# Four modulation halves moved behind layer 0's last expert, five gate tiles moved from RWKV to S5

## The chip, the cores and the metric

The kernel runs on one core of a Trainium2 chip. The metric is the device time of one execution in microseconds, as the median of several runs. The engines are TensorE (PE, with its weight loads PEld), VectorE (DVE), ScalarE (ACT), GpSimd (POOL) and SyncE (SP), which issues nearly all the transfers.

## What is computed

Two layers of a network over 256 latent tokens and 256 context tokens of width 1024, then a norm. Cut to what matters here:

```python
def hybrid_layer(x, cx, c, c_ctx, mod_w, mod_b, ...):
    mod_x = jax.nn.silu(c) @ mod_w + mod_b          # 6 chunks of 1024
    mod_c = jax.nn.silu(c_ctx) @ mod_w + mod_b
    sh1, sc1, g1, sh2, sc2, g2 = jnp.split(mod_x[:, None, :], N_MOD, axis=-1)
    px = modulate(x, norm_mix, sh1, sc1) @ w_in     # four mixers and their gates
    ...
    ys_x = [hyena_mixer(...), s5_mixer(...), rwkv_mixer(...), mamba_mixer(...)]
    x = x + g1 * merge(ys_x, gate_x, w_branch, w_out)
    x = x + g2 * moe_ffn(modulate(x, norm_ffn, sh2, sc2), *moe)
    ...                                             # the same for the context, but in the last layer

def merge(ys, gate_cols, w_branch, w_out):
    gates = jax.nn.sigmoid(gate_cols)
    out = sum(gates[..., i * D_MODEL:(i + 1) * D_MODEL] * (ys[i] @ w_branch[i]) for i in range(N_BRANCH))
    return out @ w_out
```

The modulation of a layer depends on c and c_ctx alone, so it can be computed at any time before its use. The experts (moe_ffn) are 16, of which each token uses two.

## The kernel before

Weights come as tiles of 128 x 1024 float32 (512 KB), each by one transfer of SP (`raw`, L302 to L310), and most are split into two parts for the products: ScalarE casts the high part (`wh`, L299), VectorE subtracts it for the low part (`wl`, L300), and TensorE multiplies three times (L337).

A layer runs in stages. First RWKV: its solve (`DD`, `TB`, `AB`, L499 to L530) goes level by level, with products on TensorE and masks, sums and transposes on VectorE. Then a stretch with S5, Hyena and Mamba side by side (`XX,F` are products of S5). Then the merge, the output projection, and the 16 experts, each with eight loads for `mg` and `mup` and four for `mdn`; an expert's output `yo` goes to memory (Y2) by an indirect store of GpSimd (L1419), token by token. Lists that are too long would be finished in a loop (`For_i`, L1650) whose number of turns is read at L1649; here it has none, but all engines cross it together, and SP waits for every transfer to have landed. Behind it the combine reads Y2 back and adds it to x (L1919 to L1941).

Two kinds of work are spread as fillers over the mixers. Gate tiles ("g", L1298, 32 for a layer): a tile of `w_in`, 24 products of 128x256 in layer 1, a tanh, a store. Halves of the modulation ("m", L1243 to L1273): four loads of `modw`, 16 pairs of products `raw,c`, a copy to `m` (L1251), a load of one row of `modb` into `m`, two instructions `m,rows`, an output `mo` (L1273 or L1271), a store to MR. `m` and `mo` share a tag with k.nt = 2 buffers. The order of the fillers is written out by hand:

```python
NH, NM3 = (12, 8), (0, 0)
F1 = ('g'*25+'mmm','g'*23,)
F2 = ('gm'*12,'mmmg'*4,)
```

F1 is the order beside RWKV, F2 the one beside S5, Hyena and Mamba, one entry for each layer; what is left of the 32 gates follows at the end. NH bounds the halves of a layer: 12 in layer 0 (the eight that are left of its own, and four of layer 1), 8 in layer 1. Within the windows that these strings open, the order on each engine is set by a scheduler that simulates the engines, so that a filler's products stand between those of the mixers. The experts' loads take buffers in a pattern of 19 (MST), so that a load waits for the use of the one 19 before it.

Of the kernel before, what the change touches and what calls it, by code (L numbers as in the profile page):

```python
# [8 lines left out]
F32 = mybir.dt.float32  # L9
# [9 lines left out]
D = 1024  # L19
# [5 lines left out]
# tiles of 128 columns of w_in: Hyena, S5, RWKV (r, k, v, wd | ad), Mamba (z, x, B, C), gates, then gd | dt  # L25
# [48 lines left out]
NH, NM3 = (12, 8), (0, 0)  # L74
F1 = ('g'*25+'mmm','g'*23,)
F2 = ('gm'*12,'mmmg'*4,)
NQS = (2, 4)  # pairs of groups in a part of S5
# [3 lines left out]
# ---------------------------------------------------------------- constants of the shapes  # L81


def _cst():
# [16 lines left out]
    # N^T of two-token blocks, rows s, columns t; backward scans in partitions 0..63  # L101
# [15 lines left out]
    # places less 1024  # L117
# [3 lines left out]
    # a token's row in U, and in Y2 for its first and second expert; Y2's less that of the rows without a token  # L121
    c["tok"] = np.stack([tok + 1.0, tok, tok + 512.0, tok - 1024.0], 2).reshape(128, 16)
    # resets of the running sums at the ends of 64-token chunks
# [7 lines left out]
def _rows():  # L131
    """rows of the modulation in groups of 32 (context, latent; the bias in the first's third): to each token's stream, to latent"""
    half = np.r_[np.ones(64), np.zeros(64)]
    m = np.zeros((128, 2, 128))
    for p in range(0, 128, 32):
        m[p:p + 2, 0] = half, 1 - half
        m[p + 1, 1] = 1
    m[2] = 1
    return m.reshape(128, 256)
# [39 lines left out]
def pack(inp):  # L179
    """Lays the inputs out for the loads; no arithmetic on them."""  # L180
# [32 lines left out]
    # S5: rows (second index of a pair of groups, state), columns (part, direction, pair)  # L213
# [44 lines left out]
class K:  # L258
# [13 lines left out]
    def pool(self, es, name, bufs=1):  # L272
        """a pool on the side of the parts of a layer"""
        return es.enter_context(self.tc.tile_pool(name=name, bufs=bufs, side="right", reuse_waits="tile"))
# [4 lines left out]
    def stream(self, banks="abgabgab", weights="mggg", parts="mg"):  # L279
        """banks of PSUM and buffers of weights (as loaded, and in parts) that the following program takes in turn:  # L280
        parts of a layer that run beside each other have their own"""
        self.tags, self.wtags, self.ptags = banks, weights, parts or weights
        if RESET:
            self.turn = self.wturn = 0

    def banks(self, **n):
        """the banks of PSUM by tag"""
# [9 lines left out]
    # ---- float32 operands of the large products in two parts of 12 bits: a b = ah bh + al bh + ah bl  # L297
# [4 lines left out]
    def raw(self, ap):  # L302
        """1024 columns of weights"""
# [7 lines left out]
    def wsplit(self, ap, k):  # L311
        """the parts of 1024 columns of weights (k by 1024 / k)"""
# [18 lines left out]
    def tr(self, out, in_, base=0):  # L331
        """out = in_^T on the tensor engine"""
# [6 lines left out]
    def rsqrt(self, pool, out, x, tag):  # L339
        """out = x ** -0.5 by Newton's iteration from the exponent's half; x > 0, small tiles"""  # L340
# [11 lines left out]
    def proj(self, l, t, xm, c0, c1, n=128):  # L352
        """p^T of w_in's tile t: n columns in partitions, tokens c0..c1"""
# [6 lines left out]
    # ------------------------------------------------------------------ RWKV-7  # L360
    def rwkv(self, l, xm, pc, dtT, yT, ctx_out, beside):
        """yT[:, hp, :]: the mixer's output, channels in partitions; columns 0..255 context, 256.. latent.
        dtT: Mamba's dt, from the tile that has both's columns, with tokens in partitions"""
        v, s, g, c = self.v, self.s, self.g, self.c
        with ExitStack() as es:
# [23 lines left out]
            def shifted(ps, n, j, out):  # L389
                """p + (mean of its neighbours - p) mu"""  # L390
# [20 lines left out]
            lo = {0: 64, 1: 0}  # partitions of the solves  # L411
# [4 lines left out]
            own = {d: slice(lo[d], lo[d] + 64) for d in range(2)}  # columns of a direction in the pairs' matrices  # L416
# [8 lines left out]
            for hp in range(2):  # L425
# [3 lines left out]
                # kappa: k k_k over its norm in the head  # L429
# [7 lines left out]
                # block diagonal pairs, of directions or heads: -b~ and k~ against kappa~, and the solves' (later M)  # L437
# [5 lines left out]
                for st in range(2):  # L443
# [6 lines left out]
                    for d in range(2):  # L450
                        dh = 2 * d + hp
                        # decay in log, its running sum in each chunk, and W = exp of that
# [21 lines left out]
                        s.activation(cum, cum, AF.Exp, scale=-1.0)  # 1 / W  # L474
# [16 lines left out]
                        # products of a chunk's tokens, masked: rows k~ and b~ (b~ and k~ backward)  # L491
# [11 lines left out]
                    # (I - N)^-1 of every chunk, N = -tril(kappa~ beta~^T): pairs of blocks, doubling  # L503
# [8 lines left out]
                    def each(a, b, us=range(8)):  # L512
                        """a^T b of the pairs"""
# [18 lines left out]
                    # tokens in partitions: v above (below) the solves, kappa~, and [k~; -b~]  # L532
# [33 lines left out]
                    # per chunk: H' = W_T (M H + k~^T v - b~^T u0), and y's reading of H  # L566
# [15 lines left out]
                    # the states that chunks enter (block diagonal), the last one that of the next stream's first chunk  # L582
# [23 lines left out]
                    # y^T  # L606
# [10 lines left out]
                    # group norm over a head, bonus, gate  # L617
# [24 lines left out]
    def headscale(self, pool, sq, f, eps, is_max, ni):  # L642
        """(f * sum over a head of sq, with eps added or as its least) ** -0.5, over the head's partitions"""
# [18 lines left out]
    # ------------------------------------------------------------------ conv of three taps, channels in partitions  # L662
    def conv3(self, ps, out, w3, b, c0, c1):
        """ps holds columns c0..c1 (of one or both streams)"""
# [8 lines left out]
    def silu(self, x, t):  # L673
        """x = silu(x), with a scratch like it"""
# [4 lines left out]
    # ------------------------------------------------------------------ Mamba-2  # L679
    def mamba(self, es, l, xm, pc, yT, ctx_out, dtT):  # L680
# [4 lines left out]
        if True:  # L685
# [10 lines left out]
            # softplus = max(x, 0) + log1p(exp(-|x|)); log1p(e) = 2 atanh(e / (2 + e))  # L696
# [17 lines left out]
            # running sums within a stream: forward heads 0..3, backward 4..7  # L714
# [16 lines left out]
            # weights of the context's tokens in its last state  # L731
# [6 lines left out]
            for gr in range(2):  # L738
# [8 lines left out]
                # tokens in partitions  # L747
# [10 lines left out]
                # the context's last states, [n, (direction, head, p)]  # L758
# [11 lines left out]
                for st in range(0 if ctx_out else 1, 2):  # L770
                    # C B^T by pairs of tiles, rows j, columns i; masked for each direction
# [33 lines left out]
                # + d x  # L805
                v.scalar_tensor_tensor(yT[:, gr, y0:], X[:, y0:], col("md", gr), py[:, y0:], OP.mult, OP.add)
            # times silu(z), norm over the channels
# [28 lines left out]
    def sin_of(self, pool, out, x, tag, cos=None):  # L836
        """out = sin(x), cos = cos(x): x less its whole turns, taken off in three parts"""
# [20 lines left out]
    def exp_of(self, pool, out, x, tag):  # L858
        """out = exp(x) for small tiles: 2^k times a polynomial of the rest"""
# [13 lines left out]
        # 2^k in two factors  # L873
# [8 lines left out]
    # ------------------------------------------------------------------ Hyena  # L882
    def hyena_filter(self, l, pc, pool, H):
        """H: [frequency, tile, (cos, sin), channel] of the two-sided filters"""
# [87 lines left out]
    # ------------------------------------------------------------------ S5  # L972
    def s5_params(self, l, pool):
        """[state, (part, direction, pair)]: lambda_bar, (lambda_bar - 1) / lambda, the decay over a chunk of
        4 tokens, cos and sin of the angles of a token, and of 1, 2, .. 64 chunks"""
# [44 lines left out]
    def s5_setup(self, l, a, P, tmp, TM, F, TT, ct, R):  # L1020
        """Matrices of 4-token chunks of the pairs of part a: E tokens -> state at the chunk's end, F state that
        enters -> tokens, TT within the chunk; ct: turns of the state by chunk (cos, sin), R: its decay over a chunk."""
# [940 lines left out]
```

## Time and profile before

| | before |
|---|---|
| time, median of three runs | 2172.78 us (2167.97 to 2173.02) |
| span of the profiled execution | 2165.3 us (its own time isn't listed apart) |
| TensorE busy | 1970.2 us, 11290 instructions |
| VectorE busy | 1651.0 us, 3451 instructions |
| ScalarE busy | 985.5 us, 1571 instructions |
| GpSimd busy | 399.0 us, 502 instructions |
| transfers | 406.28 MB, 188 GB/s on the mean |

Times inside the trace count from the start of the span. Layer 0's experts end near 1160, layer 1's RWKV runs from about 1210 to 1490, its S5 stretch from 1490 to 1740. "PEclk" is the share of the full TensorE clock that was granted, 1.00 for 2.4 GHz and 0.50 for 1.2. Buffers' numbers are left out in the rows, so that several tiles have one name.

### The profile page before, as it was taken

Reading aid. Unit: us, or ns where it says so; the run is one execution under the profiler, and the core shown is the slowest. Engines: PE = TensorE matmul, PEld = TensorE weight load, DVE = VectorE, ACT = ScalarE, POOL = GpSimd, SP = SyncE. Lnnn points to the kernel's source line nnn. Section 1 sums busy time; section 2 is a strip of 40 time slices with the busy share of each in tenths; the row PEclk is TensorE's granted clock in tenths of the full one; section 3 lists DMA queues with packets and bytes.
Section 4 is the critical chain, followed back from the end, with each engine's and each line's share of the span. In section 5 each row is a group of like instructions: output and inputs, shape, how many; then the busy total and the mean of one; then the engine's idle time right before and its main releaser. Section 6 shows DMA issues by size and latency. Waiting matters only on the chain. (4 is left out here: it accounts for less than half of the span.)

```text
span 2165.3 us, 31795 instructions
## 1 busy us (share of the span) xinstructions
PE 1970.2 (91%) x11290; PEld 1504.7 (69%) x11290; DVE 1651.0 (76%) x3451; ACT 985.5 (46%) x1571; POOL 399.0 (18%) x502
## 2 busy tenths in 40 slices
PE   6999999889999899999995899899798878999994
PEld 2779889567666678777774689897575767555652
DVE  5575675478888777999996686776879776888895
ACT  3321322244344234777773332323434335777783
POOL 1000100033532322102213010100524221010100
PEclk9999999889999898999998899999898988999997
DMA  7221221533444845999993221312434394899981
GB/s 299 78 74 59 74 67 52 197 123 113 156 146 154 313 172 186 362 368 372 372 341 138 84 90 63 98 52 76 160 134 161 129 350 174 304 329 366 330 325 64
DMA packets 131915, 406.28 MB, mean 188 GB/s; under 512 B 18139, under 2 KB 30205, under 8 KB 131361
## 3 DMA queue, kind: packets, MB, share of 16 engines
q1 hardware_dynamic: 125778, 388.34, 50.6%
q0 software_dynamic: 5968, 15.80, 2.3%
q8 instruction: 92, 1.51, 0.3%
q14 instruction: 77, 0.63, 0.1%
HBM read 374.72 MB, written 34.61 MB: 189 GB/s over the span
## 5 line engine op out<-in xcount | busy, mean ns | idle before, releaser
L299 ACT CAST wh<-raw 128x1024 fp32r<-128x1024 f32 x528 | 553.0, 1048 | 537.9 <-PE bank L337 482.9
L300 DVE TENSOR_TENSOR wl<-raw,wh 128x1024 fp32r<-128x1024 f32 x528 | 642.6, 1231 | 146.4 <-ACT wh L299 143.1
L337 PE MATMUL bank<-xmh,wh 128*128 128x512 f32 (+2 forms) x896 | 338.3, 378 | 15.8 <-ACT wh L299 14.7
L337 PE MATMUL bank<-xmh,wl 128*128 128x512 f32 (+2 forms) x896 | 331.0, 370 | 15.4 <-DVE wl L300 15.4
L337 PE MATMUL bank<-xml,wh 128*128 128x512 f32 (+2 forms) x896 | 326.4, 365 | 0.0
L337 PEld LDWEIGHTS bank<-xmh,wh 128*128 128x128 f32 (+1 forms) x896 | 176.7, 197 | 54.2 <-ACT wh L299 19.2
L337 PEld LDWEIGHTS bank<-xmh,wl 128*128 128x128 f32 (+1 forms) x896 | 175.9, 196 | 51.6 <-DVE wl L300 22.2
L337 PEld LDWEIGHTS bank<-xml,wh 128*128 128x128 f32 (+1 forms) x896 | 176.5, 197 | 29.2 <-issue 6.2
L337 PE MATMUL bank<-wh,xx 128*64 128x512 f32 x512 | 168.1, 397 | 0.2 <-ACT wh L299 0.2
L1419 POOL DMA_INDIRECT Y<-yo,ri x32 | 43.4, 1357 | 420.4 <-DVE yo L1418 304.8
L337 PE MATMUL bank<-DD,TB 128*128 128x64 f32 (+1 forms) x848 | 111.5, 273 | 1.3 <-DVE TB L523 0.9
L337 PEld LDWEIGHTS bank<-DD,TB 128*128 128x128 f32 x848 | 106.3, 192 | 6.0 <-DVE DD L598 0.9
L337 PE MATMUL bank<-wl,xx 128*64 128x512 f32 x256 | 102.8, 402 | 1.3 <-DVE wl L300 1.1
L337 PE MATMUL bank<-wl,hh 128*112 128x512 f32 (+1 forms) x256 | 99.9, 396 | 0.0
L337 PEld LDWEIGHTS bank<-wh,xx 128*64 128x64 f32 x512 | 69.6, 136 | 43.1 <-issue 1.4
L337 PE MATMUL bank<-wl,xh 128*112 128x512 f32 x240 | 97.9, 408 | 0.2
L337 PE MATMUL bank<-wh,hl 128*112 128x512 f32 (+1 forms) x256 | 97.4, 400 | 0.5 <-DVE hl L300 0.2
L337 PE MATMUL bank<-wh,xl 128*112 128x512 f32 x240 | 94.8, 395 | 0.9 <-DVE xl L300 0.9
L337 PE MATMUL bank<-wh,xh 128*112 128x512 f32 x240 | 92.8, 395 | 0.8 <-ACT xh L299 0.8
L337 PE MATMUL bank<-wh,hh 128*112 128x512 f32 (+1 forms) x256 | 89.8, 397 | 1.1 <-ACT hh L299 1.1
L337 PE MATMUL bank<-raw,c 128*32 128x256 f32 x768 | 71.3, 423 | 18.6 <-DMA raw<-in_modw_dram 18.6
L337 PE MATMUL bank<-DD,AB 128*128 128x64 f32 x640 | 84.5, 275 | 0.7 <-DVE DD L510 0.7
(547 smaller groups left out, 3799.5 us busy)
## 6 DMA issues: line engine op xcount, KB each, us to landing
raw<-in_mg_dram SPq DMA_DIRECT2D x128, 512.0 KB
raw<-in_mup_dram SPq DMA_DIRECT2D x128, 512.0 KB
raw<-in_mdn_dram SPq DMA_DIRECT2D x128, 512.0 KB
raw<-in_win_dram SPq DMA_DIRECT2D x112, 512.0 KB
raw<-in_modw_dram SPq DMA_DIRECT2D x96, 512.0 KB
GT<-t SPq DMA_DIRECT2D x32, 256.0 KB
raw<-in_wbr_dram SPq DMA_DIRECT2D x16, 512.0 KB
G<-GT SPq DMA_DIRECT2D x8, 1024.0 KB
```

The source lines that it names most:

```text
L299: self.s.copy(hi, src)
L300: (eng or self.v).tensor_tensor(lo, src, hi, OP.subtract)
L337: self.t.matmul(out, lhsT=lhsT, rhs=rhs, start=start, stop=stop)
L1419: g.indirect_dma_start(out=Y2, out_offset=bass.IndirectOffsetOnAxis(ap=to, axis=0), in_=yo, in_offset=None, bounds_check=1023, oob_is_err= ...
```

## The change

NM3 is now the number of halves that are computed behind the last expert of layer 0, in front of the loop; with four there, four instead of eight are left for layer 1's fillers. These are both halves of chunks 2 and 3 of layer 1's modulation. Their loads take the places of the pattern behind the experts' loads, their `m` and `mo` the two buffers of a tag in the experts' pool. Of layer 1's gate tiles 18 instead of 23 stand beside RWKV, and ten instead of four in the written order beside S5. The four reads of Y2 stand in a loop of their own ahead of the combine, and a block for NM4 halves (none) moves.

```diff
-NH, NM3 = (12, 8), (0, 0)
-F1 = ('g'*25+'mmm','g'*23,)
-F2 = ('gm'*12,'mmmg'*4,)
+NH, NM3 = (12, 8), (4, 0)
+F1 = ('g'*25+'mmm','g'*18,)
+F2 = ('gm'*12,'ggm'*4+'gg',)
...
-    def moe(self, l, m, x, pool, nt, rows, tabl, U, Y2, e_f, fp, tmp, ready, after):
+    def moe(self, l, m, x, pool, nt, rows, tabl, U, Y2, e_f, fp, tmp, ready, after, last):
...
                 for _ in prev:
                     pass
+                self.ft = tmp
+                last()
...
             nov = self.nc.values_load(cnti[0:1, 0:1], min_val=0, max_val=16)
             with self.tc.For_i(0, nov, 1) as e:
...
-                left = dict(g=32, m=NH[l] - (NM4 if last else 0))
+                left = dict(g=32, m=NH[l] - (NM4 + NM3[0] if last else 0))
...
-                if NM3[l]:
-                    k.ft = e2.enter_context(tc.tile_pool(name="md", bufs=1))
...
-                rows2 = k.moe(l, m, x, mo, nt, rows1, tabl, U, Y2, e_f, fp, tmp, ready, after)
+                rows2 = k.moe(l, m, x, mo, nt, rows1, tabl, U, Y2, e_f, fp, tmp, ready, after, lambda: some(NM3[l]))
...
-                for i in range(nt):
-                    y = tmp.tile([128, 2, D], F32, tag="y2", bufs=nt, name="y2")
+                ys = [tmp.tile([128, 2, D], F32, tag="y2", bufs=nt, name="y2") for i in range(nt)]
+                for i, y in enumerate(ys):
                     k.load(y, Y2[0:1024, :].rearrange("(k r) d -> r k d", k=2)[128 * i:128 * i + 128])
+                if not last:
+                    k.ft = tmp
+                    k.stream("g", "g", "g")
+                    some(NM4)
+                    k.stream()
+                for i, y in enumerate(ys):
```

TensorE at the end of layer 0's experts. The products with `hh` and `hl` are the last expert's, `raw,c` is a modulation load with the context vectors (x16 for a half), `m,rows` spreads a half over the tokens; TENSOR_LOAD and what follows is the loop. Before:

```order
L337 MATMUL bank<-wl,hh 112x512
L337 MATMUL bank<-wh,hl 112x512
L337 MATMUL bank<-wl,hh 112x512
L337 MATMUL bank<-wh,hl 112x512
L1649 TENSOR_LOAD cnti
L1650 COMPARE_AND_BRANCH
```

and after the change:

```order
L337 MATMUL bank<-raw,c_85 32x256 x3
L337 MATMUL bank<-wl,hh 112x512
L337 MATMUL bank<-wh,hl 112x512
L337 MATMUL bank<-wl,hh 112x512
L337 MATMUL bank<-wh,hl 112x512
L337 MATMUL bank<-raw,c_85 32x256 x6
L337 MATMUL bank<-m_10583,rows 128x512
L337 MATMUL bank<-raw,c_85 32x256 x16
L337 MATMUL bank<-m_10616,rows 128x512
L337 MATMUL bank<-raw,c_85 32x256 x16
L337 MATMUL bank<-m_10649,rows 128x512
L337 MATMUL bank<-m_10682,rows 128x512
```

Ahead of this piece, 13 and 10 more rows of `raw,c` stand among the last expert's products. So 26 rows of the modulation are now ahead of the expert's last product, and four `m,rows` ahead of the loop.

SP at the same place, where `win` are the first tiles of layer 1's projection, before:

```order
L277 DMA raw<-in_mup_dram 128x1024 x4
L277 DMA raw<-in_mdn_dram 128x1024 x4
L277 DMA raw<-in_win_dram 128x1024 x6
L1650 COMPARE_AND_BRANCH
L1650 UNCONDITIONAL_BRANCH x2
```

and after:

```order
L277 DMA raw<-in_modw_dram 128x1024 x16
L277 DMA raw<-in_win_dram 128x1024 x2
L277 DMA m_10583<-in_modb_dram 1x512
L277 DMA raw<-in_win_dram 128x1024 x2
L277 DMA MR<-mo 128x512
L277 DMA m_10616<-in_modb_dram 1x512
L277 DMA raw<-in_win_dram 128x1024 x2
L277 DMA MR<-mo 128x512
L277 DMA m_10649<-in_modb_dram 1x512
L277 DMA MR<-mo 128x512
L277 DMA m_10682<-in_modb_dram 1x512
L277 DMA MR<-mo 128x512
```

The 16 loads of the modulation come ahead of the six tiles, and four pairs of a bias load and a store between and behind these. On ScalarE the copy of the first half stands ahead of the last expert's `yo`; behind that come the casts of two of the six tiles, then the first `mo`, and from there a copy and an output in turn for the other three halves.

TensorE in the last levels of layer 1's solve, where the rows with `xmh` and `xml` are a gate tile. Before:

```order
L337 MATMUL bank<-xmh,wl 128x256
L337 MATMUL bank<-DD,TB 128x64 x4
L337 MATMUL bank<-DD,AB 128x64 x4
L337 MATMUL bank<-DD,TB 128x64 x4
L337 MATMUL bank<-DD,AB 128x64 x4
L337 MATMUL bank<-xmh,wh 128x256
L337 MATMUL bank<-xml,wh 128x256
```

and after the change:

```order
L337 MATMUL bank<-DD,TB 128x64 x4
L337 MATMUL bank<-DD,AB 128x64 x4
L337 MATMUL bank<-kr,kb 128x128 x8
L337 MATMUL bank<-DD,TB 128x64 x4
L337 MATMUL bank<-DD,AB 128x64 x4
L337 MATMUL bank<-DD,TB 128x64 x4
L337 MATMUL bank<-DD,AB 128x64 x8
L337 MATMUL bank<-DD,TB 128x64 x4
```

Five gate tiles that stood between the blocks of these levels are gone; the blocks follow each other. In the S5 stretch of layer 1 there are 14 tiles and 4 halves instead of 9 and 8; up to the second product `XX,F` some 23 tiles of 128 x 256 (gates and others) and four halves instead of 16 and eight, and behind it about one tile instead of three.

## Rows read from the trace of the kernel before

**Rows 1.** Windows: start:end, length, busy PE, PEld, DVE, ACT, POOL, PEclk, DMA share, GB/s

```profile
1060.00:1080.00 20.00, 19.78 (x97) 14.57 (x96) 19.00 (x24) 14.92 (x18) 7.37 (x2) 1.00 0.99 372
1150.00:1155.00 5.00, 2.90 (x15) 1.86 (x14) 3.68 (x5) 1.72 (x4) 0.00 (x0) 1.00 0.00 0
1160.00:1165.00 5.00, 0.00 (x0) 0.00 (x0) 1.76 (x2) 0.22 (x1) 1.17 (x1) 0.67 0.65 194
1167.00:1168.00 1.00, 0.00 (x0) 0.00 (x0) 0.00 (x0) 0.00 (x0) 0.00 (x0) 0.50 0.08 33
```

**Rows 2.** Timeline of TensorE at the end of layer 0's experts: start, duration, instruction

```profile
1158.62 0.40 PE L337 MATMUL bank<-wh,hl 128*112 128x512 f32 x1
1170.96 2.29 PE L337 MATMUL bank<-cst,n 128*128 128x128 f32 x9 [11.94 <-issue]
```

**Rows 3.** Timeline of SyncE, ScalarE, GpSimd and VectorE at the same place

```profile
1130.41 31.71 SPq L277 DMA_DIRECT2D raw<-in_win_dram  x6
...
1157.66 1.05 ACT L299 CAST wh<-raw 128x1024 fp32r<-128x1024 f32 x1 [1.73 <-PE bank L337]
...
1161.39 1.17 POOL L1419 DMA_INDIRECT Y<-yo,ri  x1 [14.50 <-DVE yo L1418]
...
1177.18 1.23 DVE L1925 TENSOR_TENSOR y<-y 128x1024 f32<-128x1024 f32 x1 [15.42 <-DMA y<-Y]
```

**Rows 4.** Window of the last levels of layer 1's solve, columns as in 1

```profile
1407.00:1446.00 39.00, 38.63 (x338) 38.08 (x337) 30.80 (x67) 5.70 (x9) 0.00 (x0) 1.00 0.22 69
```

**Rows 5.** Window of the S5, Hyena and Mamba stretch, columns as in rows 1

```profile
1630.00:1650.00 20.00, 10.43 (x65) 7.54 (x54) 19.52 (x43) 7.24 (x15) 14.37 (x23) 0.74 0.54 180
```

**Rows 6.** Waits of TensorE, 1490 to 1740: us in total, times, longest

```profile
PE bank L337 <- POOL XX L1169: 4.9, 1, 4.9
```

**Rows 7.** Timeline of TensorE, products of the modulation in a row

```profile
1532.77 1.50 PE L337 MATMUL bank<-raw,c 128*32 128x256 f32 x24
```

**Rows 8.** Groups by line, TensorE, 1490 to 1740: count, busy, mean ns, idle before

```profile
L337 PE MATMUL bank<-raw,c 128*32 128x256 f32 x256 | 22.2, 387 | 0.0
L337 PE MATMUL bank<-m,rows 128*128 128x512 f32 x16 | 9.3, 668 | 0.4 <-DMA m<-in_modb_dram 0.4
```

**Rows 9.** Timeline of one half of the modulation at full clock, layer 1

```profile
1672.84 0.57 ACT L1251 COPY m<-bank 128x512 f32<-128x512 f32 x1
...
1673.44 0.24 SPq L277 DMA_DIRECT2D m<-in_modb_dram  x1
...
1675.79 1.12 PE L337 MATMUL bank<-m,rows 128*128 128x512 f32 x2 [0.43 <-DMA m<-in_modb_dram]
...
1677.00 0.60 ACT L1273 ACTIVATE mo<-bank 128x512 f32<-128x512 f32 x1 [2.53 <-issue]
```

**Rows 10.** Timeline of one half of the modulation in layer 0

```profile
419.58 0.24 SPq L277 DMA_DIRECT2D m<-in_modb_dram  x1
...
423.47 2.08 PE L337 MATMUL bank<-m,rows 128*128 128x512 f32 x2 [0.20 <-DMA m<-in_modb_dram]
```

**Rows 11.** Window of that half, columns as in rows 1

```profile
420.00:426.00 6.00, 5.80 (x18) 2.47 (x22) 2.61 (x15) 0.36 (x1) 0.72 (x1) 0.50 0.46 136
```

**Rows 12.** Timeline of TensorE in the solve

```profile
1425.14 1.08 PE L337 MATMUL bank<-DD,TB 128*128 128x64 f32 x8
...
1428.71 0.37 PE L337 MATMUL bank<-xmh,wh 128*128 128x256 f32 x1
...
1431.19 1.00 PE L337 MATMUL bank<-DD,TB 128*128 128x64 f32 x8
```

**Rows 13.** Timeline of VectorE in the solve

```profile
1426.60 1.22 DVE L300 TENSOR_TENSOR wl<-raw,wh 128x1024 fp32r<-128x1024 f32 x1
...
1428.18 0.86 DVE L523 TENSOR_TENSOR TB<-bank,cst 64x256 f32<-64x256 f32 x2
...
1432.23 0.42 DVE L526 TENSOR_TENSOR DD<-DD,bank 128x256 f32<-128x256 f32 x1 [1.62 <-PE bank L337]
1432.69 0.45 DVE L527 STREAM_TRANSPOSE DD<-DD 128x256 f32<-128x256 f32 x1
```

More of the change, by code (lines that the diff above doesn't have):

```diff
@@ L1941, in body @@
                         operand(xm, i, y[:, 0], add=(pu[i], dg))
-                if not last:
-                    k.ft = tmp
-                    k.stream("g", "g", "g")
-                    some(NM4)
-                    k.stream()
             e_mw.close()
```

## The prediction

> **What bounds the kernel now.** I read the trace at the three places that the change touches, each time asking which wait ends last there. The first is the end of layer 0's experts. The windows [rows 1] show TensorE 2.90 us busy out of 5 from 1150 on, the DMA queues at 0.00 there, and from 1162 or so nothing on TensorE at all; from 1167 the queues are busy for 0.08 of a microsecond more, and that is the last transfer. TensorE's own rows say the same: its last product starts at 1158.62, and the next one starts at 1170.96 after 11.94 us of idle time [rows 2]. Between the two lie, in this order, the scatter of the last expert's output, issued by GpSimd at 1161.39, its landing, and the crossing of the overflow loop that every engine must make together [rows 3]. What follows is not TensorE's either: VectorE starts the combine at 1177.18, when the tokens' outputs have been read back [rows 3]. So the end of that stretch is set by the last transfer that must land before the loop, about 1167.7, and whatever lands later moves everything behind it by as much.
>
> The second place is the solve of RWKV in layer 1. From 1407 to 1446 TensorE is busy 38.63 of 39.00 us [rows 4]: it is the bound, and five gate tiles are part of that time. The third is the stretch of S5, Hyena and Mamba in layer 1, from 1490 to 1740, where TensorE is bound in some windows and VectorE in others: from 1630 to 1650 VectorE is busy 19.52 of 20 and TensorE 10.43 [rows 5], and near the end TensorE waits 4.9 us for one product of GpSimd [rows 6].
>
> **The end of layer 0's experts: four halves added.** Each half is four loads of 512 KB, 32 matmul instructions, a copy to SBUF, a load of one row of bias over the copy, two matmul instructions with "rows", a copy out and a store to MR. The loads first: there are 16, they stand on SP between the last expert's weights and layer 1's first tiles, and the queues are empty from 1150 to 1155 [rows 1], while SP's six win loads before needed 31.71 us, because they waited for buffers [rows 3]. I take the 16 loads as hidden. Their cover is this idle DMA time; without it each would cost about 1.4 us (estimate: 512 KB at the 372 GB/s of the experts [rows 1]).
>
> The matmuls are not all hidden. The order puts 13 + 10 + 3 = 26 of a half's 16 rows (52 instructions) before the last expert's last product. 24 instructions of this kind took 1.50 us in a row [rows 7], so 52 take 3.2 us; by the busy time of 22.2 us for 256 [rows 8] they would take 4.5. I take 3.2: TensorE ends at about 1162.2 instead of 1159.0, and the scatter lands about 3 us later. If the rest were covered, that would be the whole cost of this place.
>
> The rest is a chain, and this is the largest term. The halves share two buffers for the copy m and the output mo, so that they go through one after the other: copy, bias, rows, output. At full speed I read one turn from 1672.84 to the end of mo at 1677.60, 4.76 us: the copy 0.57, the bias from 1673.44 to the start of its reader at 1675.79 (2.35), the rows 1.12, the output 0.60 [rows 9]. TensorE has little else to do by then, and its clock falls when it idles: the granted clock was 0.67 on the mean from 1160 to 1165 and 0.50 at 1167 [rows 1], which is the 1.2 GHz level; at 0.50 the same rows took 2.08 us instead of 1.12 [rows 10, 11], so a turn takes 5.7 us. The upper end is that turn of layer 0, beside a busier queue: its bias took from 419.58 to 423.47, 3.89 us, and the whole turn 0.6 + 3.89 + 2.08 + 0.6 = 7.2 us [rows 10].
>
> The Trainium skill ("TensorE: Matmul & The Clock Gate", section "HAM oscillation — how this bites in real kernels") says that matmuls whose groups are separated by waits for a DMA start at the low clock again and again. The rows at 0.50 agree with it; by the rule all turns are at 5.7, without it they are at 4.76, which is 3 us less in the sum.
>
> Where does the chain start? The first copy can follow the first half's products, near 1159.5. But on ScalarE the first output stands behind the casts of two of layer 1's tiles. The later of these waits for a buffer that TensorE frees when it has read the seventh modulation load (rows 25 to 28 of 64), near 1162.3; a 512 KB load then takes about 1.4 + 2.35 us (estimate from that rate and from the bias load), the cast 1.05 [rows 3], the output 0.60. So the first output is there at about 1168, three turns of 5.7 follow, the last store is issued at 1185 and lands 2.35 us later (the bias load's time, the nearest row that I have for the store): 1187.5 instead of 1167.7. **Cost +19.** The lower end takes the start from the copies (1159.5 + 4 x 4.76 + 2.35 = 1180.9, +13), the upper end takes 7.2 for each turn (1168 + 21.6 + 2.35, +24). Behind it are late: the crossing of the loop, the read of the tokens' outputs, and the combine.
>
> The Trainium skill ("DMA: Bandwidth & Descriptors", section "🔬 Anatomy of one DMA — SWDGE (gpsimd) path") gives any DMA a fixed cost of about 2.0 us, however small, most of it the receipt of the write. The bias of 2 KB, 2.35 us on another path, is of that kind; by the page's figure the three turns and the store would be 1.4 us cheaper.
>
> **Layer 1's RWKV: five gate tiles removed.** A tile is 24 products. 20 of them stand from 1428.71 to 1431.19 between the blocks of the solve, 0.12 us each, so that a tile is 2.9 us; the solve's four blocks for one level take 3.57 (1425.14 to 1428.71) [rows 12]. Five tiles are 5 x 2.9 = 14.4 us of TensorE. As the engine is busy 38.63 of 39.00 [rows 4], all of that could come back, but without the gates the solve is a chain between TensorE and VectorE: a block of TB, 0.86 for its mask, a block of AB, 0.42 for the sum and 0.45 for the transpose [rows 13], with the two blocks at 0.89 (a quarter of 3.57): 3.5 us and four hand-overs, which I put at 4.0 per level against 3.57 of products. The seven levels of this stretch ((39 - 14.4) / 3.57) then take 28 us instead of 39. **Gain -11.** Ends: -14.4 (only TensorE; VectorE's 30.80 less five splits of 1.22 is 24.7 and would allow it [rows 4, 13]) and -8 (4.5 per level).
>
> **Layer 1's S5 stretch: five tiles come, four halves go.** Added on TensorE 14.4 us, on VectorE 5 x 1.22 = 6.1. Removed on TensorE: 256 instructions and 16 of rows cost 22.2 + 9.3 us for eight halves [rows 8], so four are at most 15.8, and 4 x (1.94 + 1.16) = 12.4 by the row of 24 [rows 7]. So the sum is +2 on TensorE. But VectorE is the bound in part of this stretch [rows 5], halves cost it nothing there and gates do, so up to +6 more; and by the order the gate tiles come earlier: 23 instead of 16 ahead of the second XX,F product, and one instead of three after it, so that some fall into its 4.9 us of waiting [rows 6], which would give back that and the two tiles. **+3**, between -6 and +9. Grouping the four reads of Y ahead of the combine leaves the order as it was: 0.
>
> **Sum.** 19 - 11 + 3 = +11 us, against the profiled span of 2165.3: 2176. The median of the runs shown is 2172.8, 7.5 above that span, and so 2183.5.
>
> **Rivals.** (a) The chain is covered: the halves' copies run from 1159.5 as soon as they can, the store lands within the scatter's flight, and the place costs only the 3.2 us of the scatter. That decides if the last store lands before about 1171. Then 3 - 11 + 0 = -8: 2165, faster than before (the S5 stretch at 0, between its ends). For it: the scatter alone takes 6 us to land and the engines are idle then. Against it: four turns of 4.76 are 19 us, and only 11 are free. (b) Layer 1 gives more than I count: TensorE runs dry of 14.4 us in the solve and the S5 stretch absorbs the tiles (-4), while the chain costs 16: -2, about 2170, no change. For it: TensorE's work in layer 1 falls by about 12 us in sum, and it is the bound in the solve [rows 4]. (c) The solve was as much VectorE's chain as TensorE's: removing gates returns 4 to 6 us, and S5 pays +6: +19 + 1 = 2193. Against it: the sum DD waited for TensorE 1.62 us at 1432.23 [rows 13].
>
> **How the numbers follow.** My forecast has 0.42, (a) 0.13, (b) 0.25, (c) 0.20. About 0.3%, 6.5 us, is what a measurement of this kernel can tell from no change. The forecast's own bounds run from 2174 to 2190, so it gives a quarter of itself to no change at most; (b) is nearly all no change, with a little to faster. Faster 0.16, same 0.27, slower 0.57. The range reaches from (b)'s lower part to (c): 2167 to 2194, leaving out most of (a) and what lies beyond (c).
>
> **What would show it.** In the trace after: four m, mo turns between 1160 and 1190, each near 5.7 us, with TensorE idle around them and the granted clock at 0.50; the next product of TensorE after the loop near 1190 instead of 1170.96; the solve without gates at 4.0 us a level and VectorE nearly as busy as TensorE; between 1490 and 1740 a stretch about 3 us longer. It is wrong if the last store lands before 1176, if a level still takes 4.5 or more, or if the S5 stretch gets shorter.

## The result

The changed kernel took 2198.4 us (median of four runs, 2193.9 to 2200.0), the kernel before 2171.1 beside it; the ratio is 1.0118, with a 95% interval from 1.0102 to 1.0134. It is 27 us slower, where the forecast was 11 us slower: the sign was right, the size was not, and the time lies above the range. The profiled execution's span is 2192.0 us against 2165.3. Three executions of the experiments below, one of b19 and two of ba20, took 3287 to 4801 us and are left out of all medians.

I cut both traces at the same instructions: the first transpose `cst,h` of layer 0's last expert on TensorE (L334, it turns the hidden values for the down projection; the texts call it the last expert's first product), the first instruction of the combine on VectorE, the first `dg,y` product of TensorE (the start of layer 1), the last product `Q` (the end of RWKV), and the end of the span.

| | before | after | |
|---|---|---|---|
| last expert's first product | 1152.0 | 1153.1 | +1.1 |
| from there to the combine | 25.2 | 43.4 | +18.2 |
| combine to `dg,y` | 24.2 | 24.2 | 0 |
| `dg,y` to the last `Q` (RWKV) | 284.8 | 297.1 | +12.3 |
| last `Q` to the end (S5 stretch and all behind) | 679.1 | 674.2 | -4.9 |
| span | 2165.3 | 2192.0 | +26.7 |

**The end of layer 0's experts** costs about what the forecast said. The timeline of the changed kernel there, all engines (start, duration, instruction, idle time before it and what ended that), answering to [rows 2, 3, 9]:

```profile
1161.38 0.59 ACT L1251 COPY m<-bank 128x512 f32<-128x512 f32 x1 [2.31 <-PE bank L337]
...
1166.05 0.94 POOL L1419 DMA_INDIRECT Y<-yo,ri  x1 [18.06 <-DMA raw<-in_win_dram]
...
1169.61 0.59 ACT L1273 ACTIVATE mo<-bank 128x512 f32<-128x512 f32 x1
...
1173.13 2.05 PE L337 MATMUL bank<-m,rows 128*128 128x512 f32 x2 [3.16 <-DMA m<-in_modb_dram]
...
1175.22 0.60 ACT L1273 ACTIVATE mo<-bank 128x512 f32<-128x512 f32 x1 [4.54 <-PE bank L337]
...
1178.09 1.10 PE L337 MATMUL bank<-m,rows 128*128 128x512 f32 x2 [0.55 <-DMA m<-in_modb_dram]
1179.22 0.60 ACT L1273 ACTIVATE mo<-bank 128x512 f32<-128x512 f32 x1 [2.93 <-PE bank L337]
...
1183.25 0.60 ACT L1273 ACTIVATE mo<-bank 128x512 f32<-128x512 f32 x1 [2.96 <-PE bank L337]
1183.88 0.33 SPq L277 DMA_DIRECT2D MR<-mo  x1
...
1189.09 9.38 PE L337 MATMUL bank<-cst,n 128*128 128x128 f32 x64 [5.87 <-issue]
...
1196.52 1.22 DVE L1931 TENSOR_TENSOR y<-y 128x1024 f32<-128x1024 f32 x1 [25.56 <-DMA y<-Y]
```

The four outputs `mo` start at 1169.61, 1175.22, 1179.22 and 1183.25, the last store is issued at 1183.88, TensorE starts again at 1189.09 (before: 1170.96) and the combine at 1196.52 (before: 1177.18). Between them TensorE has almost nothing to do.

**The solve of RWKV in layer 1** is where the sum went wrong. Windows of the changed kernel (columns as in rows 1: after the length the busy time of PE, PEld, DVE, ACT, POOL, then the granted clock, the DMA share and GB/s):

```profile
1422.00:1428.00 6.00, 5.56 (x51) 5.33 (x50) 4.68 (x10) 1.33 (x2) 0.00 (x0) 1.00 0.31 109
1428.00:1430.00 2.00, 0.13 (x2) 0.00 (x0) 1.94 (x6) 0.00 (x0) 0.00 (x0) 0.69 0.00 0
1430.00:1432.00 2.00, 1.60 (x8) 1.63 (x8) 1.89 (x4) 0.00 (x0) 0.00 (x0) 0.50 0.00 0
1440.00:1460.00 20.00, 20.00 (x96) 20.00 (x96) 9.80 (x24) 0.00 (x0) 0.00 (x0) 0.50 0.00 1
...
1480.00:1482.00 2.00, 2.00 (x20) 2.00 (x20) 0.96 (x3) 0.69 (x2) 0.00 (x0) 1.00 0.00 0
```

TensorE ran at full clock until 1428, waited, and came back at 0.50, the 1.2 GHz level. From 1440 to 1460 it is busy 20.00 of 20.00 us, and the clock stays at 0.50; the low stretch goes on to 1480. TensorE's rows say what a block costs there:

```profile
1427.07 1.06 PE L337 MATMUL bank<-DD,AB 128*128 128x64 f32 x8
1430.40 1.94 PE L337 MATMUL bank<-DD,TB 128*128 128x64 f32 x8 [2.27 <-DVE TB L523]
...
1435.55 1.92 PE L337 MATMUL bank<-DD,TB 128*128 128x64 f32 x8
1437.25 1.91 PE L337 MATMUL bank<-DD,AB 128*128 128x64 f32 x8
```

It waits 2.27 us for the mask TB of VectorE; from then on a block of eight instructions takes 1.71 us, start to start (1435.55 to 1437.25), and a level of four blocks 6.8 us, against the 3.57 of [rows 12]. In the kernel before, a gate tile stood from 1410.42 on behind the `kr,kb` products, and TensorE went from it to the next block without a wait. The float32 products from 1446 on, blocks among them, had no gate tile beside them and kept the clock:

```profile
1408.78 1.71 PE L337 MATMUL bank<-kr,kb 64*128 64x128 f32 x16
1410.42 0.39 PE L337 MATMUL bank<-xmh,wh 128*128 128x256 f32 x1
...
1412.92 1.00 PE L337 MATMUL bank<-DD,TB 128*128 128x64 f32 x8
```

```profile
1446.00:1458.00 12.00, 11.91 (x108) 11.64 (x108) 5.97 (x14) 5.08 (x11) 1.21 (x2) 1.00 0.04 12
```

### The profile page after: what moved, and what is told of

The parts are those of the page before. It is cut to its first block, busy times and chain, and to the rows that moved or that the text cites. A ratio compares the mean times of both kernels' runs of the same rounds, so it can differ in the third digit from the quotient of the medians.

```text
span 2192.0 us, 31798 instructions
## 1 busy us (share of the span) xinstructions
PE 1990.3 (91%) x11290; PEld 1527.8 (70%) x11290; DVE 1652.9 (75%) x3451; ACT 990.0 (45%) x1573; POOL 401.5 (18%) x502
## 5 line engine op out<-in xcount | busy, mean ns | idle before, releaser
L337 PE MATMUL bank<-DD,TB 128*128 128x64 f32 (+1 forms) x848 | 123.7, 293 | 3.8 <-DVE TB L523 3.4
L337 PEld LDWEIGHTS bank<-DD,TB 128*128 128x128 f32 x848 | 118.1, 210 | 8.8 <-issue 2.6
L1419 POOL DMA_INDIRECT Y<-yo,ri x32 | 43.2, 1350 | 424.7 <-DVE yo L1418 308.2
L337 PE MATMUL bank<-DD,AB 128*128 128x64 f32 x640 | 97.1, 302 | 3.6 <-DVE DD L510 3.6
L337 PEld LDWEIGHTS bank<-DD,AB 128*128 128x128 f32 x640 | 90.8, 218 | 4.3 <-DVE DD L510 3.4
```

Of the source, the lines that this page charges most:

```text
L337: self.t.matmul(out, lhsT=lhsT, rhs=rhs, start=start, stop=stop)
L1419: g.indirect_dma_start(out=Y2, out_offset=bass.IndirectOffsetOnAxis(ap=to, axis=0), in_=yo, in_offset=None, bounds_check=1023, oob_is_err= ...
```

## The experiments

The first question was which part of the change costs the 12 us in RWKV, and whether the wait at 1428 is its cause. In all tables and texts "RWKV" is the stretch from `dg,y` to the last `Q`, "tail" that from the last expert's first product to the combine, "rest" that from the last `Q` to the end. Times are medians of several executions, the three stretches are from one profiled execution each, and that one may lie off the median: tail_only's took 2175.8 us, fill6r4's 2190.0, ba20's 2169.4.

| | time, us | ratio to before, 95% | tail | RWKV | rest |
|---|---|---|---|---|---|
| before | 2169 to 2171 | | 25.2 | 284.8 | 679.1 |
| changed | 2198.4 | 1.0102 to 1.0134 | 43.4 | 297.1 | 674.2 |
| tail_only | 2181.7 | 1.0041 to 1.0088 | 43.2 | 286.3 | 670.4 |
| gates_only | 2223.0 | 1.0206 to 1.0279 | 25.0 | 304.8 | 714.3 |
| ag19 | 2171.1 | 0.9999 to 1.0025 | 43.4 | 274.9 | 674.3 |
| nobias | 2201.9 | 1.0114 to 1.0172 | 38.9 | 300.8 | 682.2 |
| fill6 | 2199.1 | 1.0119 to 1.0180 | 43.5 | 298.8 | 676.9 |
| b19 | 2207.7 | 1.0157 to 1.0232 | 24.9 | 295.7 | 704.3 |
| b20 | 2175.5 | 1.0011 to 1.0044 | 25.1 | 278.2 | 689.5 |
| nobias19 | 2190.0 | 1.0057 to 1.0121 | 37.4 | 297.7 | 677.3 |
| fillr12 | 2202.7 | 1.0138 to 1.0197 | 42.8 | 301.2 | 678.0 |
| fill62 | 2176.4 | 1.0021 to 1.0052 | 43.8 | 273.7 | 677.2 |
| fill6r4 | 2179.9 | 1.0025 to 1.0059 | 45.5 | 278.8 | 684.1 |
| ba20 | 2177.4 | 1.0015 to 1.0057 | 40.6 | 282.1 | 665.4 |

### The two parts apart

tail_only, against the changed kernel:

```diff
-F1 = ('g'*25+'mmm','g'*18,)
-F2 = ('gm'*12,'ggm'*4+'gg',)
+F1 = ('g'*25+'mmm','g'*23,)
+F2 = ('gm'*12,'mmmg'*4,)
```

> The change with layer 1's fillers in the old order (23 gate tiles beside RWKV): the four halves stay behind the last expert, nothing is taken from the solve. Theory (the solve without tiles lost TensorE's clock): the first combine instruction of VectorE after the loop stays near 1196 as in the changed kernel, RWKV from the first dg,y product to the last Q product takes 285 us as before (297 in the changed kernel) at a granted clock of 1.00 in the solve, and the S5 stretch loses 6 to 12 us with four halves fewer: 2171 + 19 - 9 = 2181. Rival (the low clock of layer 1 comes from the moved halves, which shift layer 1 by 19 us against something): RWKV takes 297 us here too, time near 2193.

Measured: 2181.7; RWKV 286.3, 1.5 more than before; the tail 43.2; the rest 8.7 us shorter than before. The clock is low once in the solve, for some 7 us from a wait of 3.15 us for DD on, and 1.00 after that:

```profile
1412.00:1419.00 7.00, 5.44 (x25) 5.44 (x26) 5.95 (x12) 0.83 (x2) 2.08 (x2) 0.52 0.25 78
1419.00:1507.00 88.00, 86.21 (x743) 82.37 (x742) 56.25 (x146) 21.78 (x46) 3.84 (x6) 1.00 0.12 40
```

The changed kernel has the same short stretch, from 1415 to 1422; the kernel before has none. So the moved halves cost 18 us behind the last expert, return up to 9 in layer 1 (the profiled execution was 6 us faster than the median), and bring the short low stretch. The long one is not theirs.

gates_only, against the changed kernel:

```diff
-NH, NM3 = (12, 8), (4, 0)
+NH, NM3 = (12, 8), (0, 0)
```

> The change without the four halves behind the last expert: 18 gate tiles beside RWKV, 14 tiles and eight halves beside S5. Theory: the tail is that of the kernel before (next TensorE product at 1171), RWKV takes 297 us with a granted clock of 0.50 for some 45 us of the solve, the S5 stretch grows by 8 to 14 us: 2171 + 12 + 11 = 2194. Rival (the clock falls because of the moved halves): RWKV takes 285 - 11 = 274 us at full clock, time 2171 - 11 + 11 = 2171.

Measured: 2223.0, with RWKV at 304.8 and a granted clock of 0.50 from 1414 to 1472. That settles that moving the gates alone makes the clock fall. The wait is another one here: 2.91 us for TB at 1413.40, ahead of the `kr,kb` products. The time is 29 us above what I expected; about 8 of that are in RWKV, and the rest (714.3) is 35 longer than before, where I had put 11. The order F2 has places for four halves only, and four more are left for the end, behind the mixers, where nothing stands beside them. TensorE there, with the idle time before each:

```profile
1776.67 2.05 PE L337 MATMUL bank<-m,rows 128*128 128x512 f32 x2 [6.11 <-DMA m<-in_modb_dram]
...
1796.36 1.22 PE L337 MATMUL bank<-yh,wh 128*128 128x256 f32 x4 [14.07 <-ACT wh L299]
```

20 us of waits in these two rows alone. So this kernel shows the fall of the clock, but not the price of the gate tiles in the S5 stretch.

### One gate tile back

ag19, against the changed kernel; the tile comes to stand behind the `kr,kb` products, where TensorE had waited:

```diff
-F1 = ('g'*25+'mmm','g'*18,)
+F1 = ('g'*25+'mmm','g'*19,)
```

> The changed kernel with one gate tile more beside RWKV, 19 instead of 18; by the order it stands just where TensorE waited in the changed kernel before the clock fell (1427 to 1430). After it the solve's blocks are alone, 13 levels. Theory A (the wait lets the clock fall, and the blocks alone hold a clock that is high but do not raise one that is low): the granted clock stays at 1.00 through the blocks, a level takes 3.6 to 4.0 us, RWKV takes about 276 us, time 2198 - 20 = 2178. Theory B (blocks alone can't hold the clock for long, whatever stood ahead of them): the clock falls to 0.50 within some 15 us of the last tile, a level takes 6.8 us, RWKV takes 291 to 296, time near 2195.

Measured: 2171.1, so that one tile is worth 27 us, and RWKV takes 274.9 us, 10 less than before. TensorE in the solve of this kernel:

```profile
1431.20 1.10 PE L337 MATMUL bank<-DD,AB 128*128 128x64 f32 x8 [0.18 <-DVE DD L510]
1432.49 1.08 PE L337 MATMUL bank<-DD,TB 128*128 128x64 f32 x8 [0.18 <-DVE TB L523]
...
1438.04 1.06 PE L337 MATMUL bank<-DD,TB 128*128 128x64 f32 x8
1438.94 1.06 PE L337 MATMUL bank<-DD,AB 128*128 128x64 f32 x8
```

and its window:

```profile
1440.00:1460.00 20.00, 20.00 (x182) 20.00 (x181) 18.81 (x45) 0.23 (x1) 0.00 (x0) 1.00 0.00 1
```

The waits are 0.18 us, and from there on the blocks stand alone for 30 us at full clock, 0.89 us a block: theory A. Blocks alone hold the clock. It is not one lucky execution: the ten of ag19 took 2169 to 2177 us, the four of the changed kernel 2194 to 2200. VectorE is busy 18.81 of 20.00, so that here it is nearly as late as TensorE; the level is 3.57 us, not the 4.0 of the forecast.

b19, against the kernel before; here the 19th tile comes to stand one level too early, and the place behind `kr,kb` stays open:

```diff
-F1 = ('g'*25+'mmm','g'*23,)
+F1 = ('g'*25+'mmm','g'*19,)
```

> The kernel before with 19 gate tiles beside RWKV instead of 23 and nothing else; by the order the 19th tile stands one level too early, and the place behind the kr,kb products is open as in the changed kernel. Theory (the wait): the clock falls to 0.50 at that place, a level takes 6.8 us, RWKV takes 290 to 300 us instead of 285, time 2170 + 10 + 3 = 2183. Rival (number of tiles, 19 are enough; or the moved halves are needed for the fall): the clock stays at 1.00, RWKV takes 275 us, time 2170 - 10 + 3 = 2163.

Measured: RWKV 295.7. As many tiles as in ag19, and the clock falls. TensorE's row at that place, with its wait:

```profile
1413.42 1.06 PE L337 MATMUL bank<-DD,AB 128*128 128x64 f32 x8
1416.51 1.94 PE L337 MATMUL bank<-DD,TB 128*128 128x64 f32 x8 [2.03 <-DVE TB L523]
```

So it is where a tile stands, not how many there are. The time is 2207.7, 25 us above my number, because the rest grew by 25 us: nine tiles are left for the end of the S5 stretch instead of five, and TensorE's waits between 1770 and 1820 (us in total, times, longest) are for the casts of weights at the end of that stretch:

```profile
PE bank L337 <- ACT wh L299: 21.2, 3, 16.1
```

b20 is b19 with 20 tiles; by the order the 20th stands behind `kr,kb`.

> The kernel before with 20 gate tiles beside RWKV instead of 23; by the order the 20th stands behind the kr,kb products. Theory (the wait): it is covered, the clock stays at 1.00, RWKV loses three tiles at 2.5 us each, 277 us instead of 285, the S5 stretch pays 0 to 4 us: 2170 - 7.5 + 2.5 = 2165, faster than the kernel before. Rival (the blocks alone lose the clock in any case where many stand together): RWKV takes 290 us or more, time 2175 or more.

Measured: the clock holds and RWKV takes 278.2, as the theory says; but the rest grows by 10 us and the time is 2175.5, slower than before. My price of 2.5 us for three more tiles at the end of the S5 stretch was wrong: in the old order of fillers, tiles that are left over are not covered.

### Is it the wait?

fill6, against the changed kernel, in front of the second solve (nobody reads the products):

```diff
+                    if l == 1 and hp == 1 and st == 1:
+                        ps = self.bank()
+                        for i in range(6):
+                            self.mm(ps[:, 0:256], self.ident, KR[:, 0, 0:2].rearrange("p c d t -> p (c d t)"))
                     DD = tile("DD", 2, 8, 64)
```

> The changed kernel, 18 gate tiles beside RWKV, with six products more (identity with kr, 128x256 float32, nobody reads them) in the second solve of layer 1, by the order right behind the kr,kb products, where TensorE waited from 1427 to 1430 in the changed kernel. Theory (the wait lets the clock fall, and the solve's blocks alone hold a high clock): the granted clock stays at 1.00 through the blocks, a level takes 3.6 us, RWKV takes 273 to 276 us instead of 297, time 2198 - 24 = 2174 or a little less. Rival (the tile itself matters, or 18 tiles are too few): the clock falls, RWKV takes 297 us, time near 2198.

Measured: no gain, 2199.1. The clock fell at 1433, four us later than in the changed kernel. TensorE:

```profile
1426.86 2.86 PE L337 MATMUL bank<-kr,cst 128*128 128x256 f32 x12
...
1431.85 1.08 PE L337 MATMUL bank<-DD,AB 128*128 128x64 f32 x8 [0.41 <-DVE DD L514]
1432.95 1.93 PE L337 MATMUL bank<-DD,TB 128*128 128x64 f32 x8
1434.67 1.91 PE L337 MATMUL bank<-DD,AB 128*128 128x64 f32 x8
```

The twelve instructions `kr,cst` fill the long wait, but 0.41 us are left ahead of the next pair's first block, and right behind that block the next ones take 1.71 us. This could be the short wait, or it could be that float32 products are not what holds the clock. Three runs told these apart. fillr12 has twelve fp32r products of a gate tile's kind at the first place:

```diff
+                        for i in range(12):
+                            self.mm(ps[:, 0:256], xm[0][:, i % KT, 0:128], xm[0][:, i % KT, L:2 * L])
```

> The changed kernel (18 gate tiles) with twelve products more that nobody reads, fp32r 128x256 as in a gate tile, behind the kr,kb products of layer 1's second solve; the short wait of 0.4 us after the next blocks stays open. Theory C (float32 work counts for little in what holds the clock, a gate tile's fp32r products count for much; a wait among float32 work alone lets it fall): the clock stays at 1.00, a level takes 3.6 us, RWKV takes 273 us instead of 297, time about 2172. Theory D (any wait at that place lets it fall, whatever stood ahead of it, unless it is under 0.2 us): the clock falls at about 1432 as in fill6, time near 2198.

Measured: 2202.7, the clock falls.

```profile
1426.41 1.69 PE L337 MATMUL bank<-xmh 128*128 128x256 f32 x12
...
1432.09 1.43 PE L337 MATMUL bank<-DD,TB 128*128 128x64 f32 x8 [2.26 <-DVE TB L527]
1433.31 3.62 PE L337 MATMUL bank<-DD,AB 128*128 128x64 f32 x16
```

The twelve products moved the wait, they did not fill it: VectorE's mask comes later too, the block that needs it starts at 1432.09 (1430.40 in the changed kernel), and TensorE waits 2.26 us for it. So fp32r work ahead of a wait did not save the clock here. fill62 is fill6 with two more float32 products at the second place:

```diff
                     v.transpose(fl(DM), fl(DT))
+                    if l == 1 and hp == 1 and st == 1:
+                        ps = self.bank()
+                        for i in range(2):
+                            self.mm(ps[:, 0:256], self.ident, fl(DT)[:, 0:256])
```

> The changed kernel with the six float32 products of fill6 behind the kr,kb products, and two more (identity with DD) ahead of the second pair's first block, so that the short wait of fill6 at 1431.4 shrinks too. Theory C (float32 work does not hold the clock where a wait stands in it): it falls unless the wait is gone entirely; I expect 0.2 us of wait left and a fall, time near 2198. Theory D (waits alone): no wait over 0.2 us is left, the clock stays at 1.00, time about 2174.

Measured: 2176.4; RWKV 273.7, the shortest of all, with the clock at 1.00 for the whole solve.

```profile
1433.21 1.08 PE L337 MATMUL bank<-DD,cst 128*128 128x256 f32 x4
1434.13 1.00 PE L337 MATMUL bank<-DD,AB 128*128 128x64 f32 x8
1434.97 1.06 PE L337 MATMUL bank<-DD,TB 128*128 128x64 f32 x8
```

```profile
1434.00:1464.00 30.00, 30.00 (x271) 29.98 (x270) 27.90 (x66) 1.18 (x2) 0.00 (x0) 1.00 0.00 1
```

No wait is left, and float32 work alone held the clock: TensorE is busy 30.00 of 30.00 us. Theory C is out, theory D holds at this place: what decides is whether TensorE waits there. Against fill6 the difference is 0.41 us of waiting and 25 us of RWKV. The two products that close that wait are work as well, and this pair of runs can't tell the missing wait from the added work.

fill6r4 is fill6 with four fp32r products of that kind at the second place.

> The changed kernel with the six float32 products of fill6 behind the kr,kb products, and four fp32r products of 128x256 ahead of the second pair's first block, at the short wait of fill6. Both theories: the clock stays at 1.00 if four fp32r products and a short wait are enough, time about 2174, RWKV 274 us. If it falls all the same, more fp32r work than four products is needed, and fillr12 and the run with 19 tiles say how much is enough.

Measured: 2179.9, RWKV 278.8, the clock holds; its profile has a second low stretch, ahead of the first solve (0.53 from 1284 to 1298), which I can't explain. It agrees with fill62: four fp32r products at the second place do what two float32 ones do.

### The chain behind the last expert

nobias, against the changed kernel, for the four halves behind the last expert, which so lack their bias:

```diff
-        if bias is None:
+        if bias is None and not self.tail:
             self.load(m4[2:3], self.i["modb"][l, 2 * j + h:2 * j + h + 1, :])
```

> The changed kernel without the four loads of the bias row behind the last expert; these four halves of the modulation lack their bias. Theory (the halves go through one serial chain, which sets the crossing of the loop): each turn loses the bias load's 2.0 to 2.4 us but for the first, whose output waits for a tile of the next layer anyway; the first combine instruction comes 6 to 9 us earlier than 1196.5, time 2198 - 7 = 2191. Rival (the crossing waits for the loads and stores of the queue, not for the chain): less than 2 us.

Measured: the tail is 38.9 us instead of 43.4, 4.5 less where I expected 6 to 9, so that the chain does set the crossing of the loop. The outputs and the combine in its timeline:

```profile
1171.75 0.60 ACT L1274 ACTIVATE mo<-bank 128x512 f32<-128x512 f32 x1 [1.81 <-PE bank L338]
...
1175.08 0.60 ACT L1274 ACTIVATE mo<-bank 128x512 f32<-128x512 f32 x1 [2.14 <-PE bank L338]
...
1181.99 0.60 ACT L1274 ACTIVATE mo<-bank 128x512 f32<-128x512 f32 x1 [1.22 <-PE bank L338]
...
1195.55 1.23 DVE L1933 TENSOR_TENSOR y<-y 128x1024 f32<-128x1024 f32 x1 [16.55 <-DMA y<-Y]
```

The last output starts 25.4 us behind the last expert's first product (1156.64), before 30.2 (1183.25 less 1153.08). The time didn't fall, 2201.9: RWKV, with its clock low, took 300.8, and the rest 682. A place whose clock falls is a poor scale for 5 us, and I repeated it with 19 tiles:

> The changed kernel with 19 gate tiles, and without the four loads of the bias row behind the last expert (these four halves lack their bias): the serial chain's price, where the solve is at full clock as in the run with 19 tiles (2171.1). Theory (the chain sets the crossing of the loop): from the last expert's first product to the combine 39 us instead of 43.4, time 2171 - 4.5 = 2166.6. Rival (the profiles differ in that place for another reason, the chain is covered): time 2171 as with the loads.

Measured: the tail is 37.4 us, six less. But the leaner chain changed the order in layer 1, the 19th tile stood elsewhere, TensorE waited 2.27 us for TB behind `kr,kb`, and the clock fell again: RWKV 297.7, time 2190.0. The tail's price is shown, the time it would give is not.

ba20 is the changed kernel with 20 tiles and the bias loaded ahead into a row of its own:

```diff
+            mb1 = self.mbt.tile([1, 512], F32, tag="mb1", bufs=2, name="mb1")
+            self.load(mb1, self.i["modb"][l, 2 * j + h:2 * j + h + 1, :])
+            bias = (self.one, mb1)
```

> The changed kernel with 20 gate tiles beside RWKV, and the bias of the four halves behind the last expert loaded ahead into a row of its own and added by a product, so that no load stands in the chain of copy, rows and output. Theory (the chain sets the crossing of the loop): a turn takes 3.3 to 3.8 us instead of 5.0, the combine starts 5 us earlier, 38 us behind the last expert's first product instead of 43.4; RWKV at full clock takes 277 us; time 2171 + 2.5 - 5 = 2168, against 2171 with 19 tiles. Rival (the chain is covered by other waits there): 2173 or more.

Measured: the tail is 40.6, 2.8 less, where I expected 5. RWKV took 282.1, with the clock low for 4 us (0.57 from 1423 to 1427, after a wait of 1.43 us and with a gate tile following), and the time is 2177.4. No kernel here beats the one before: with the chain shortened, the four halves still cost 12 to 15 us behind the last expert and return 9 at most.

## Why the prediction was wrong

**The tail was right in its mechanism, and in size by some luck.** Forecast +19 (its own terms give 1187.5 less 1167.7, that is 19.8), measured +18.2. The first output came at 1169.6 to 1170.2 (forecast 1168). The scatter was issued 4.7 us later, not 3: 1.1 of that lies ahead of the last expert's transposes, and the modulation's products cost 1.91 + 1.49 + 0.63 us among the expert's, nearer to the 4.5 that I had set aside than to my 3.2, and a break of some 0.4 us at each change. The turns were 5.6, 4.0 and 4.0 us where I took 5.7 for all: in the second, `m,rows` took 2.05 us, but behind the last half's 32 products the clock was back, and the row at 1178.09 took 1.10. So the rule of the Trainium skill ("TensorE: Matmul & The Clock Gate", section "HAM oscillation — how this bites in real kernels"), as I applied it, held for one turn of three. The three turns took 13.6 us instead of 17.1, which made up for the late first output. The last store was issued at 1183.9 (forecast 1185), and TensorE started again at 1189.1 (forecast near 1190). nobias shows that it is this chain. Rival (a) is out.

**The solve was wrong in sign, and this is the step that failed.** Forecast -11, measured +12.3. The step read TensorE as busy 38.63 of 39.00 us [rows 4] and took each product's duration as given, so that removing 14.4 us of products could only save time, up to what the chain with VectorE allows. But the tiles did a second thing: they stood where TensorE would else have waited for VectorE, and so they kept its clock. With 18 tiles the wait behind `kr,kb` is open (2.27 us), the clock falls to 0.50, and seven levels' worth of blocks, from 1432 to 1480, run at nearly double price: 48 us for what takes 25 at 3.57 a level. That is the 23 us between -11 and +12. Where the clock was held, the gain was there: -9.9 in ag19 with four tiles removed, -11.1 in fill62 with five. So the size of -11 was right for a solve at full clock, and by luck: a level takes 3.57 us and not 4.0, the products that fill the waits eat the difference. Rival (c), VectorE's chain, has no part in it either: in the low stretch VectorE is busy 9.80 of 20.00 us.

I had the rule in hand and applied it to the tail alone. In the solve I looked at the busy share, where I should have asked of every removed tile what TensorE does in its place at that moment, wait or work.

**The S5 stretch and the rest** came out at -4.9 where I said +3, within my ends of -6 and +9; but a shorter stretch was one of my own signs of being wrong, as was a level of 4.5 us or more (6.8 measured). tail_only splits it, as far as one profiled execution of each tells: four halves less return 8.7 us, so that five tiles more in the new order of fillers cost 3.8. I had priced the halves by TensorE's 12.4 us and the tiles by 14.4; both were covered in part.

**The sum.** 1.1 + 18.2 + 12.3 - 4.9 = 26.7. The range ended at 2194 because none of the cases had the clock of the solve in it; (b) and (c) argued about who is late in the solve at a given clock.

## To carry to other kernels

Work that fills an engine's waits may be worth more than its own time: before it is moved away, ask what TensorE does at each place where it stood, and look at the granted clock of the stretches around, not only at the busy share. A place that waits 2 us can cost 24 us if what follows can't bring the clock back; then one tile, or a few products that nobody needs, at that place is cheap. And small serial steps (copy, bias, product, output, store) in front of a point that all engines cross together are paid for, however idle the engines are.

## What the hardware showed

The granted clock does not follow the busy share. In the changed kernel TensorE is busy 20.00 of 20.00 us at 0.50, and for 48 us the solve's float32 blocks of 128x64 don't bring the clock back; it was back right behind eight transposes `cst,kr` and `cst,kb` (L334), at 1480. The same blocks hold a clock of 1.00 for 30 us (ag19, fill62). Earlier, at 1416, the clock of the changed kernel was low too, after a wait of 3.16 us, and it was back by 1422, in the course of 22 products of a gate tile. The Trainium skill ("TensorE: Matmul & The Clock Gate", section "🔬 Part 1: The HAM clock gate (the "warmup" mystery)") gives the full clock to an engine that has been busy for a while; the rows of the changed kernel from 1432 to 1480 differ from that, and here they decide.

How short a wait must be is not settled. With 0.41 us between float32 blocks the clock fell (fill6), with 0.18 us twice, behind fp32r products, it held (ag19), with none it held (fill62). But the length alone does not decide: in ba20 TensorE waited 0.80 us for TB at 1475.52, between float32 products of 128x128 and a block, and the clock stayed at 1.00.

```profile
1475.52 1.10 PE L338 MATMUL bank<-DD,TB 128*128 128x64 f32 x8 [0.80 <-DVE TB L524]
```

```profile
1470.00:1500.00 30.00, 27.77 (x248) 25.84 (x245) 15.47 (x55) 7.13 (x17) 1.94 (x3) 1.00 0.01 2
```

Whether the fp32r products near it count in ag19 stays open, as does why the blocks can't raise the clock that they can hold.
